# Gates, branch products and the merged sum of a three-layer block with tokens on the partitions

## The chip, the cores and the metric

The kernel runs on one core of a Trainium2 chip, as one program from load to store. Its time is device microseconds from the launch to the end of that core. Three runs are shown; the time of the kernel is their median. The profile is one more execution, in which every instruction of each engine was recorded: TensorE (PE, its weight loads PEld), VectorE (DVE), ScalarE (ACT), GpSimd (POOL) and SyncE (SP, which issues the DMAs).

## What is computed

256 tokens of width 1024 go through two layers of one kind and one of another. Each layer ends its mixing part in the same way: three branches of width 512, each multiplied by a branch matrix to width 1024, weighted by a sigmoid gate of width 1024 that is itself a product of the hidden state with columns of the input matrix, summed, and multiplied by an output matrix. Cut to that:

```
# layers 0 and 1 (hybrid_layer), h = rms_norm(x, ln_mix)
merge = (h @ w_in)[..., 3368:]                        # 3 x 1024 columns
gates = sigmoid(merge.reshape(B, S, 3, D) + b_merge)
merged = (gates[:, :, 0] * (o_nsa @ w_branch[0])
          + gates[:, :, 1] * (o_gla @ w_branch[1])
          + gates[:, :, 2] * (o_mem @ w_branch[2]))
x = x + merged @ w_out                                # then an MLP of width 4096

# layer 2 (hybrid_layer_2), h = x, no bias in the gates
gates = sigmoid((x @ w_in)[..., 5120:].reshape(B, S, 3, D))
mixed = sum over 3 branches of gates * (y @ w_branch)
out = layer_norm(ALPHA * x + mixed @ w_out, ln_g, ln_b)
```

All is float32. o_nsa, o_gla and o_mem are the results of a sparse attention, a gated linear attention and an attention over 256 memory tokens.

## The kernel before, in words

**Precision and weights.** Every large product is made from three float32r matmuls: each operand is split into a high and a low part, and high x high, high x low and low x high are summed in PSUM. Activations keep their parts in hh and hl (hidden state), oh and ol (branch results), mg (the merged sum). Weights arrive by DMA on SP's queue into one of four raw buffers of 1024 elements per partition (512 KB); `unit` (L441) issues the DMA, and `split` (L429) makes hi on ScalarE (L435; each sixth on POOL, L433) and lo on VectorE (L439). There are four hi and four lo buffers, so three units can lie ready while PE uses one.

**Two forms of a product.** `tok_major` (L489) has tokens on the partitions of the result: for each k (128 rows of the contraction) and each of the two token tiles, 128 tokens of the activation are stationary and up to 512 weight columns move; the two results fill two PSUM banks (acc, four in all). `transposed` (L503) has output columns on the partitions: for each of two blocks of 128 columns and each k, the 128 x 128 block of weights is stationary and the 256 tokens move; two blocks fill one PSUM bank. In the trace every matmul of both is at L188, the helper that records it; transposes are at L192.

**Order.** PE's order is written out by the program itself. A planned clock (clock, advanced at L187 and L191 by 1.69 or 0.425 ns per moving column) stands for PE's time. The attention parts are generators ("chains", L130 to L153) that yield the planned nanoseconds until their next step; `pump` runs those that are due after every three matmuls of `tok_major` or every six of `transposed`, so that their matmuls fall between those of the large products. `need` (L157) runs chains until a given k of an activation has been produced. The other engines' orders come from the framework's scheduler, and all semaphores too.

**The stage of the change.** For each branch (in layers 0 and 1 in the order 2, 1, 0) `gates_of` (L1125) makes the gate with four calls of `transposed`, each 256 columns: VectorE multiplies by the tokens' norm factor RB, laid along the free axis (L1130), and ScalarE does tanh with a bias per partition, CBH (L1134). Then `merge_branch` (L1137) makes the branch product in the same form. The first branch writes (gate + 1) x product into M (L1147); the later ones multiply in place (L1149) and POOL adds to M (L1150). In the last branch each quarter of M is split at once into mg by `hilo` (L522: high on ScalarE L527, low on VectorE L528), which the output projection `out_proj` (L1155) takes as its stationary operand: there output columns of M must lie on the partitions. In layer 2 (L1579 to L1593) the gate is a tanh straight from PSUM (L1585). There is one gate buffer and one M buffer.

Of the kernel before, what the change touches and what calls it, by code (L numbers as in the profile page):

```python
# [98 lines left out]
def block_kernel(ctx, tc, x_in, mem_in, positions, ln_mix, w_in, b_merge, nsa_q_norm, nsa_k_norm,  # L99
# [173 lines left out]
    def load_rows():  # L273
# [3 lines left out]
        rows(48, 48, b_merge.rearrange("l b (k p) -> (l b k) p", p=P))  # L277
# [53 lines left out]
    CBH = consts.tile([P, 48], F32, name="CBH")  # L331
# [4 lines left out]
    def late_cols():  # L336
        pt = PS()
        tr(pt[:, :128], ROWB, IDF)
        dve.tensor_copy(COL[:, 48:128], pt[:, 48:128])
        dve.memset(COL[0:16, 102:110], 1.0)  # L340
        dve.memset(COL[64:80, 102:110], 1.0)
        dve.tensor_scalar(CBH, COL[:, 48:96], 0.5, None, op0=OP.mult)
# [120 lines left out]
    def units(w2d, r0, nk, cols, paired=None, fine=False):  # L463
        n = sum(c1 - c0 for c0, c1 in cols)
        if paired:
            c0, c1 = cols[0]
            srcs = [(slice(64 * j, 64 * j + 64), 0, n,
                     w2d[256 * j:256 * j + 256, c0:c1].rearrange("(a d) n -> d a n", d=64)) for j in range(2)]
            h, lo = unit(srcs, 4, n)
            return [(h[:, j, :], lo[:, j, :]) for j in range(4)]  # L470
        per = max(1, 1024 // n)
# [17 lines left out]
    def tok_major(hh, hl, w2d, r0, nk, cols, fine=False):  # L489
        n = sum(c1 - c0 for c0, c1 in cols)  # L490
        ps = [ACC(), ACC()]
        ws = units(w2d, r0, nk, cols, None, fine)
# [26 lines left out]
    def v2(ps):  # L519
        return ps.rearrange("p (a b) -> p a b", a=2)  # L520
# [604 lines left out]
    def gates_of(l, b, hh, hl, RB):  # L1125
        g = B8("gate")
        for c in range(4):
            ps = transposed(hh, hl, w_in[l], 0, 8, 3368 + 1024 * b + 256 * c, ACC())
            tmp = T2("gtmp", (2, 256))
            dve.tensor_tensor(tmp, v2(ps), RB[:, None, :].to_broadcast([P, 2, 256]), op=OP.mult)  # L1130
            for j in range(2):
                cb = 2 * c + j
                bc = l * 24 + b * 8 + cb
                act(g[:, cb, :], tmp[:, j, :], AF.Tanh, scale=0.5, bias=CBH[:, bc:bc + 1])  # L1134
        return g

    def merge_branch(w2d, oT, g, M, last, mg, rows=None):  # L1137
        oh, ol = oT
        first = M is None
        if first:  # L1140
            M = B8("M")
        for c in range(4):
            ps = transposed(oh, ol, w2d, 0, 4, 256 * c, ACC(), rows)
            cs = slice(2 * c, 2 * c + 2)
            fl = lambda t: t[:, cs, :].rearrange("p a b -> p (a b)")
            if first:
                dve.scalar_tensor_tensor(fl(M), fl(g), 1.0, ps, op0=OP.add, op1=OP.mult)  # L1147
            else:
                dve.scalar_tensor_tensor(fl(g), fl(g), 1.0, ps, op0=OP.add, op1=OP.mult)  # L1149
                pool.tensor_tensor(fl(M), fl(M), fl(g), op=OP.add)  # L1150
                if last:
                    hilo(fl(mg[0]), fl(mg[1]), fl(M), 0.5)
# [525 lines left out]
```

## Time and profile before

| | |
|---|---|
| time, median of 3 runs | 1257.58 us (1254.6, 1257.58, 1258.07) |
| profiled execution, from its first to its last instruction | 1254.4 us |
| PE busy | 1234.7 us, 98% |
| DVE busy | 846.5 us, 67% |
| ACT busy | 596.6 us, 48% |
| POOL busy | 244.6 us, 19% |
| read from HBM | 208.74 MB, 167 GB/s over the span |

The profiled execution's span runs from its first to its last instruction and lies 3.2 us under the median. Layer 0 begins near 80 us, its gates near 145; its merge ends at 288.9 and the output projection starts there. Layer 1 has its gates from about 625 to 772, layer 2 from 1116 to 1227. A matmul's printed duration is longer than the distance from one to the next, because matmuls overlap; how fast PE goes is read from the starts.

### The profile page before, as it was taken

The page shows a single profiled execution, that of the slowest core. Times are in us where ns is not written, and L with a number is a line of the kernel's source. Part 1 is how long each engine was busy: PE and PEld are TensorE (multiplying, and loading weights), DVE is VectorE, ACT ScalarE, POOL GpSimd, SP SyncE. Part 2 cuts the span into 40 slices and gives each one's busy share as a digit, 9 for nine tenths or more (in the row PEclk, how much of TensorE's full clock was granted, in tenths as well). Part 3 has the DMA queues.
Part 4 walks back from the last instruction along what each step waited for, and adds up shares of the span by engine and source line. Part 5 has one row for each costly group of instructions (what it writes and reads, how often), then busy time and mean ns, then how long its engine had stood idle before and what let it go on. Part 6 is the DMA issues. An engine that isn't in the chain of part 4 may idle for free.

```text
span 1254.4 us, 21138 instructions
## 1 busy us (share of the span) xinstructions
PE 1234.7 (98%) x8317; PEld 1108.0 (88%) x8317; DVE 846.5 (67%) x1356; ACT 596.6 (48%) x956; POOL 244.6 (19%) x246
## 2 busy tenths in 40 slices
PE   8999999999999999999999999999999999999997
PEld 6897799998899899888799998989998988899996
DVE  5867878566754545567978566654545899956756
ACT  6567544444644444556644434544434343453532
POOL 2300320122112112200320023121211122111213
PEclk9999999999999999999999999999999999999999
DMA  8557533466566666656623566565665654445562
GB/s 269 177 157 203 155 101 102 137 185 199 185 185 185 189 183 196 184 153 173 191 68 112 155 167 190 177 193 179 198 187 171 202 155 137 153 135 169 179 219 74
DMA packets 165559, 211.00 MB, mean 168 GB/s; under 512 B 12065, under 2 KB 132277, under 8 KB 165460
## 3 DMA queue, kind: packets, MB, share of 16 engines
q1 hardware_dynamic: 165172, 209.49, 55.9%
q8 instruction: 65, 1.06, 0.3%
q0 software_dynamic: 288, 0.16, 0.1%
q14 instruction: 34, 0.28, 0.1%
HBM read 208.74 MB, written 1.05 MB: 167 GB/s over the span
## 4 chain that ended last, share of the span: by engine, by line
PE 84%; DVE 8%; POOL 2%; ACT 2%; issue 2%; DMA 0%; SPq 0%; POOLq 0%; ACTq 0%; DVEq 0%
PE acc L188 59%; PE psm L188 18%; PE psm L192 3%; PE pso L188 3%; DVE lo L439 3%; DVE b8x L1435 2%; POOL M L1150 2%; ACT hi L435 1%; PE acc L782 1%; ACT b8x L527 1%; DVE gate L1149 0%; DVE b8x L528 0%; DVE QB L1046 0%; ACT pexp L920 0%; DMA gtmp<-in_mem_norm 0%
## 5 line engine op out<-in xcount | busy, mean ns | idle before, releaser
L439 DVE TENSOR_TENSOR lo<-raw,hi 128x1024 fp32r<-128x1024 f32 (+1 forms) x359 | 451.5, 1261 | 264.0 <-ACT hi L435 203.5
L435 ACT ACTIVATE hi<-raw 128x1024 fp32r<-128x1024 f32 (+1 forms) x314 | 330.0, 1057 | 415.4 <-PE acc L188 254.7
L188 PE MATMUL acc<-hh,hi 128*128 128x256 f32 x960 | 278.7, 290 | 0.4 <-ACT hi L435 0.4
L188 PE MATMUL acc<-hh,lo 128*128 128x256 f32 x960 | 272.0, 283 | 1.7 <-DVE lo L439 1.6
L188 PE MATMUL acc<-hl,hi 128*128 128x256 f32 x960 | 271.9, 283 | 0.0
L188 PEld LDWEIGHTS acc<-hh,hi 128*128 128x128 f32 x960 | 184.0, 192 | 4.1 <-issue 2.5
L188 PEld LDWEIGHTS acc<-hh,lo 128*128 128x128 f32 x960 | 184.0, 192 | 2.3 <-DVE lo L439 2.3
L188 PEld LDWEIGHTS acc<-hl,hi 128*128 128x128 f32 x960 | 184.1, 192 | 1.1 <-DVE hl L528 0.2
L433 POOL TENSOR_SCALAR hi<-raw 128x1024 fp32r<-128x1024 f32 x55 | 67.0, 1219 | 477.8 <-PE acc L188 319.7
L188 PE MATMUL psm<-hh,hi 128*128 128x256 f32 x448 | 126.8, 283 | 0.0
L188 PE MATMUL psm<-hh,lo 128*128 128x256 f32 x448 | 126.8, 283 | 0.0
L188 PE MATMUL psm<-hl,hi 128*128 128x256 f32 x448 | 126.8, 283 | 0.0
L188 PE MATMUL acc<-hi,b8x 128*128 128x512 f32 (+1 forms) x336 | 104.0, 384 | 0.1
L188 PE MATMUL acc<-hi,oh 128*128 128x512 f32 x256 | 100.2, 391 | 0.0
L188 PE MATMUL acc<-lo,oh 128*128 128x512 f32 x256 | 99.8, 390 | 0.0
L188 PE MATMUL acc<-hi,ol 128*128 128x512 f32 x256 | 99.6, 389 | 0.0
L188 PE MATMUL acc<-hi,hh 128*128 128x512 f32 (+1 forms) x224 | 90.0, 402 | 0.0
L188 PE MATMUL acc<-lo,hh 128*128 128x512 f32 (+1 forms) x224 | 84.8, 378 | 2.2 <-DVE lo L439 2.2
L188 PEld LDWEIGHTS psm<-hl,hi 128*128 128x128 f32 x448 | 86.0, 192 | 0.5
L188 PEld LDWEIGHTS psm<-hh,hi 128*128 128x128 f32 x448 | 86.0, 192 | 0.5
L188 PEld LDWEIGHTS psm<-hh,lo 128*128 128x128 f32 x448 | 86.0, 192 | 0.0
L188 PE MATMUL acc<-hi,hl 128*128 128x512 f32 (+1 forms) x224 | 84.8, 378 | 0.0
(369 smaller groups left out, 2151.5 us busy)
## 6 DMA issues: line engine op xcount, KB each, us to landing
raw<-in_w_in SPq DMA_DIRECT2D x160, 512.0 KB
raw<-in_w_up SPq DMA_DIRECT2D x64, 512.0 KB
raw<-in_w_down SPq DMA_DIRECT2D x64, 512.0 KB
raw<-in_w_branch SPq DMA_DIRECT2D x28, 512.0 KB
raw<-in_w_out SPq DMA_DIRECT2D x24, 512.0 KB
raw<-in_cmp_w SPq DMA_DIRECT2D x32, 256.0 KB
raw<-in_mem_w_kv SPq DMA_DIRECT2D x15, 512.0 KB
raw<-in_w_branch SPq DMA_DIRECT2D x16, 256.0 KB
```

The lines of the kernel that those rows point to most:

```text
L188: nc.tensor.matmul(o, l, r, start=start, stop=stop, skip_group_check=True)
L192: nc.tensor.transpose(o, i, ident)
L433: pool.tensor_scalar(hi, raw, 1.0, 1.0, op0=OP.mult, op1=OP.mult)
L435: act(hi, raw, AF.Copy)
L439: dve.tensor_tensor(lo, raw, f32(hi), op=OP.subtract)
L527: act(hi, src, AF.Copy, scale=scale)
L782: nc.tensor.matmul(ph[32 * j:32 * j + 32, k * 256:k * 256 + 256], R[k][:, lp].rearrange("p a b -> p (a b)"), rv[:, j, :], start=q == 0, st ...
L1150: pool.tensor_tensor(fl(M), fl(M), fl(g), op=OP.add)
L1435: dve.scalar_tensor_tensor(CV[:, cb], GLU[:, cb, t:t + 256], CWT[:, cb, t:t + 1], CV[:, cb], op0=OP.mult, op1=OP.add)
```

## The change

Gates, branch products and M get the form of `tok_major`: tokens on the partitions, two halves of 512 columns instead of four calls of 256. `units` cuts the paired rows of the last branch's matrix into two units per half, so that units keep their size of 1024 elements. `gates_of` now takes the norm factor per partition (rsd) and loads b_merge, the same row for all 128 partitions and both token tiles, by a DMA on POOL's queue into the gate buffer itself; VectorE multiplies the PSUM by rsd and adds it in one step, and ScalarE does tanh in place. CBH and the rows of b_merge at the start go. In the last branch VectorE adds to M instead of POOL, and a new chain, `merged_transposed`, transposes each half of M on PE (four blocks of 128 x 128 per token tile) and splits it from PSUM into mg; `out_proj` finds through `need` which k of mg are planned. Layer 2 has the same, without bias.

```diff
     def units(w2d, r0, nk, cols, paired=None, fine=False):
         n = sum(c1 - c0 for c0, c1 in cols)
+        per = max(1, 1024 // n)
         if paired:
             c0, c1 = cols[0]
-            srcs = [(slice(64 * j, 64 * j + 64), 0, n,
-                     w2d[256 * j:256 * j + 256, c0:c1].rearrange("(a d) n -> d a n", d=64)) for j in range(2)]
-            h, lo = unit(srcs, 4, n)
-            return [(h[:, j, :], lo[:, j, :]) for j in range(4)]
-        per = max(1, 1024 // n)
+            res = []
+            for k in range(0, 4, per):
+                srcs = [(slice(64 * j, 64 * j + 64), 0, n,
+                         w2d[256 * j + 64 * k:256 * j + 64 * (k + per), c0:c1].rearrange("(a d) n -> d a n", d=64))
+                        for j in range(2)]
+                h, lo = unit(srcs, per, n)
+                res += [(h[:, j, :], lo[:, j, :]) for j in range(per)]
+            return res
...
-    def gates_of(l, b, hh, hl, RB):
-        g = B8("gate")
-        for c in range(4):
-            ps = transposed(hh, hl, w_in[l], 0, 8, 3368 + 1024 * b + 256 * c, ACC())
-            tmp = T2("gtmp", (2, 256))
-            dve.tensor_tensor(tmp, v2(ps), RB[:, None, :].to_broadcast([P, 2, 256]), op=OP.mult)
-            for j in range(2):
-                cb = 2 * c + j
-                bc = l * 24 + b * 8 + cb
-                act(g[:, cb, :], tmp[:, j, :], AF.Tanh, scale=0.5, bias=CBH[:, bc:bc + 1])
+    def gates_of(l, b, hh, hl, rsd):
+        g = B8("gate", shape=(2, 1024))
+        nc.gpsimd.dma_start(g, wrap(b_merge[l, b], [[0, P], [0, 2], [1, 1024]]))
+        for h in range(2):
+            hs = slice(512 * h, 512 * h + 512)
+            c0 = 3368 + 1024 * b + 512 * h
+            ps = tok_major(hh, hl, w_in[l], 0, 8, [(c0, c0 + 512)])
+            for tt in range(2):
+                gs = g[:, tt, hs]
+                dve.scalar_tensor_tensor(gs, ps[tt], rsd[:, tt:tt + 1], gs, op0=OP.mult, op1=OP.add)
+                act(gs, gs, AF.Tanh, scale=0.5)
         return g
+
+    def merged_transposed(M, h, mg, prog):
+        yield 1500.0
+        for tt in range(2):
+            pt = PS()
+            for j in range(4):
+                tr(pt[:, j * P:j * P + P], M[:, tt, 512 * h + j * P:512 * h + j * P + P], IDF)
+            ks, ts_ = slice(4 * h, 4 * h + 4), slice(tt * P, tt * P + P)
+            hilo(mg[0][:, ks, ts_], mg[1][:, ks, ts_], v4(pt), 0.5)
+            if tt == 0:
+                yield 800.0
+        prog[0] = 4 * h + 4
 
     def merge_branch(w2d, oT, g, M, last, mg, rows=None):
         oh, ol = oT
         first = M is None
         if first:
-            M = B8("M")
-        for c in range(4):
-            ps = transposed(oh, ol, w2d, 0, 4, 256 * c, ACC(), rows)
-            cs = slice(2 * c, 2 * c + 2)
-            fl = lambda t: t[:, cs, :].rearrange("p a b -> p (a b)")
-            if first:
-                dve.scalar_tensor_tensor(fl(M), fl(g), 1.0, ps, op0=OP.add, op1=OP.mult)
-            else:
-                dve.scalar_tensor_tensor(fl(g), fl(g), 1.0, ps, op0=OP.add, op1=OP.mult)
-                pool.tensor_tensor(fl(M), fl(M), fl(g), op=OP.add)
-                if last:
-                    hilo(fl(mg[0]), fl(mg[1]), fl(M), 0.5)
+            M = B8("M", shape=(2, 1024))
+        prog = [0]
+        if last:
+            ready[id(mg[0])] = (mg[0], prog)
+        for h in range(2):
+            hs = slice(512 * h, 512 * h + 512)
+            ps = tok_major(oh, ol, w2d, 0, 4, [(512 * h, 512 * h + 512)], False, rows)
+            for tt in range(2):
+                gs, ms = g[:, tt, hs], M[:, tt, hs]
+                if first:
+                    dve.scalar_tensor_tensor(ms, gs, 1.0, ps[tt], op0=OP.add, op1=OP.mult)
+                else:
+                    dve.scalar_tensor_tensor(gs, gs, 1.0, ps[tt], op0=OP.add, op1=OP.mult)
+                    (dve if last else pool).tensor_tensor(ms, ms, gs, op=OP.add)
+            if last:
+                start(merged_transposed(M, h, mg, prog))
         return M
...
         for bi, b in enumerate((2, 0, 1)):
-            g = B8("gate")
-            for c in range(4):
-                ps = transposed(hh, hl, w, 0, 8, 5120 + 1024 * b + 256 * c, ACC())
-                act(g[:, 2 * c:2 * c + 2, :], v2(ps), AF.Tanh, scale=0.5)
+            g = B8("gate", shape=(2, 1024))
+            for h in range(2):
+                c0 = 5120 + 1024 * b + 512 * h
+                ps = tok_major(hh, hl, w, 0, 8, [(c0, c0 + 512)])
+                for tt in range(2):
+                    act(g[:, tt, 512 * h:512 * h + 512], ps[tt], AF.Tanh, scale=0.5)
```

## Rows read from the trace of the kernel before

**Rows 1.** Part 1 of the page: busy time of each engine, its share of the span and its instructions.

```profile
PE 1234.7 (98%) x8317; PEld 1108.0 (88%) x8317; DVE 846.5 (67%) x1356; ACT 596.6 (48%) x956; POOL 244.6 (19%) x246
```

**Rows 2.** Busy time by stretch, in the stages of the change. Columns: the stretch, its length, then busy us (and instructions) of PE, PEld, DVE, ACT and POOL, the granted clock as a share of full, the share of the DMA engines, GB/s.

```profile
160.00:202.90 42.90, 42.53 (x321) 38.81 (x321) 34.99 (x88) 20.79 (x46) 8.49 (x14) 0.96 0.33 99
...
242.97:279.90 36.93, 36.93 (x310) 36.93 (x310) 22.93 (x22) 15.64 (x21) 8.85 (x6) 1.00 0.63 171
...
1151.00:1214.00 63.00, 63.00 (x527) 63.00 (x527) 41.89 (x44) 27.73 (x35) 11.45 (x8) 1.00 0.57 180
```

**Rows 3.** Who waited for whom over the whole span: total us, times, the longest. The first row is PE's largest, the second ScalarE's.

```profile
PE acc L188 <- DVE lo L439: 4.1, 4, 2.2
...
ACT hi L435 <- PE acc L188: 254.7, 149, 8.5
```

**Rows 4.** PE in order of time at the start of layer 0's output projection: start, us, what. "x2" is two matmuls taken together.

```profile
296.83 0.93 PE L188 MATMUL acc<-hi,b8x 128*128 128x512 f32 x2
297.60 0.40 PE L188 MATMUL acc<-lo,b8x 128*128 128x512 f32 x1
297.99 0.73 PE L188 MATMUL acc<-hi,b8x 128*128 128x512 f32 x2
298.56 0.39 PE L188 MATMUL acc<-lo,b8x 128*128 128x512 f32 x1
```

**Rows 5.** The chain of work that ended last, in order of time: start, us, engine, result, line and matmuls of an unbroken run. In this order: 512 moving columns (mem_kv and layer 0), 256 columns (gates of layer 0), 256 columns (MLP), 512 columns (MLP).

```profile
49.92 10.93 PE acc L188 x48
...
242.97 36.95 PE acc L188 x308
...
372.92 11.51 PE psm L188 x96
384.44 10.91 PE acc L188 x48
```

**Rows 6.** Groups of instructions by line and form: the branch products of three layers, one of their three matmuls.

```profile
L188 PE MATMUL acc<-oh,hi 128*128 128x256 f32 x288 | 83.1, 288 | 0.0
```

**Rows 7.** The same chain in order of time: four transposes between matmuls.

```profile
304.19 0.44 PE psm L192 x4
```

**Rows 8.** Groups of instructions by line and form: engine, out<-in, count, busy us and mean ns of one, idle time before and its releaser. Evacuations of gates and products, the adds to M, the split of M, and the splits of weights.

```profile
L439 DVE TENSOR_TENSOR lo<-raw,hi 128x1024 fp32r<-128x1024 f32 x353 | 445.6, 1266 | 260.8 <-ACT hi L435 200.3 <-POOL hi L433 59.0
...
L1150 POOL TENSOR_TENSOR M<-M,gate 128x512 f32<-128x512 f32 x24 | 43.2, 1802 | 90.8 <-DVE gate L1149 85.2 <-ACT hi L435 5.5
...
L1134 ACT ACTIVATE gate<-gtmp,CBH 128x256 f32<-128x256 f32 x48 | 22.2, 501 | 12.5 <-DVE gtmp L1130 12.4
...
L1130 DVE TENSOR_TENSOR gtmp<-acc,RB 128x512 f32<-128x512 f32 x24 | 16.4, 684 | 0.9 <-PE acc L188 0.9
L1149 DVE SCALAR_TENSOR_TENSOR gate<-gate,acc 128x512 f32<-128x512 f32 x24 | 16.3, 680 | 6.9 <-PE acc L188 6.9
...
L528 DVE SCALAR_TENSOR_TENSOR b8x<-M,b8x 128x512 fp32r<-128x512 f32 x12 | 9.4, 787 | 16.6 <-ACT b8x L527 16.6
...
L527 ACT ACTIVATE b8x<-M 128x512 fp32r<-128x512 f32 x12 | 7.6, 632 | 31.4 <-POOL M L1150 31.4
...
L1298 DVE TENSOR_TENSOR X<-X,acc 128x512 f32<-128x512 f32 x8 | 5.1, 679 | 0.0
```

**Rows 9.** DMAs that POOL issues, from the list of DMA issues (KB each, median us from issue to landing), and two single microseconds of layer 2 by stretch (columns as in rows 2).

```profile
DM<-const_d POOLq DMA_DIRECT2D x1, 96.0 KB, 4.4
...
CBT<-const_b POOLq DMA_DIRECT2D x1, 64.0 KB, 5.5
```

```profile
1216.00:1217.00 1.00, 1.00 (x11) 1.00 (x10) 1.00 (x1) 0.00 (x0) 0.97 (x1) 1.00 0.77 193
...
1218.00:1219.00 1.00, 1.00 (x11) 1.00 (x10) 1.00 (x3) 0.67 (x1) 0.00 (x0) 1.00 1.05 406
```

**Rows 10.** Layer 0, chains between gate matmuls, in order of time: PE from 155 to 182, then VectorE's steps that it reads, then two stretches of layer 0 and layer 1 (columns as in rows 2).

```profile
155.19 3.64 PE L188 MATMUL psm<-KB,b8x 128*128 128x16 f32 x32
...
159.36 0.28 PE L188 MATMUL acc<-hl,hi 128*128 128x256 f32 x1
159.48 0.28 PE L188 MATMUL acc<-hh,lo 128*128 128x256 f32 x1
...
161.84 0.41 PE L188 MATMUL acc<-hl,hi 128*128 128x256 f32 x1
162.05 0.41 PE L188 MATMUL acc<-hh,lo 128*128 128x256 f32 x1
...
176.88 0.82 PE L192 MATMUL psm<-CF,pexp 128*128 128x128 f32 x6
178.06 0.68 PE L188 MATMUL psm<-QB,b8x 128*128 128x128 f32 x4 [0.37 <-DVE a L1059]
...
181.98 0.76 PE L188 MATMUL pso<-pts,n 128*64 128x256 f32 x3
```

```profile
176.96 0.60 DVE L925 TENSOR_SCALAR pexp<-pexp,r 128x256 f32<-128x256 f32 x2
...
179.57 0.55 DVE L940 COPY pts<-psm 128x384 f32<-128x384 f32 x1
```

```profile
160.00:180.00 20.00, 19.63 (x143) 18.15 (x143) 17.42 (x49) 8.91 (x25) 7.67 (x12) 0.92 0.24 80
640.00:660.00 20.00, 20.00 (x161) 18.78 (x159) 19.07 (x52) 10.22 (x26) 7.24 (x12) 1.00 0.31 96
```

More of the change, by code (lines that the diff above doesn't have):

```diff
@@ L275, in rows @@
             nc.sync.dma_start(ROWB[r0:r0 + n, :], src)
-        rows(48, 48, b_merge.rearrange("l b (k p) -> (l b k) p", p=P))
         rows(96, 2, gla_norm)
@@ L330, in block_kernel @@
     dve.tensor_copy(COL[:, 32:48], pt[:, 32:48])
-    CBH = consts.tile([P, 48], F32, name="CBH")
     GQK = consts.tile([P, 2], F32, name="GQK")
@@ L338, in late_cols @@
         tr(pt[:, :128], ROWB, IDF)
-        dve.tensor_copy(COL[:, 48:128], pt[:, 48:128])
+        dve.tensor_copy(COL[:, 96:128], pt[:, 96:128])
         dve.memset(COL[0:16, 102:110], 1.0)
         dve.memset(COL[64:80, 102:110], 1.0)
-        dve.tensor_scalar(CBH, COL[:, 48:96], 0.5, None, op0=OP.mult)
         dve.tensor_tensor(GQK, COL[:, 98:100], COL[:, 100:102], op=OP.mult)
@@ L487, in units, with tok_major @@
         return res
-    def tok_major(hh, hl, w2d, r0, nk, cols, fine=False):
+    def tok_major(hh, hl, w2d, r0, nk, cols, fine=False, paired=None):
         n = sum(c1 - c0 for c0, c1 in cols)
         ps = [ACC(), ACC()]
-        ws = units(w2d, r0, nk, cols, None, fine)
+        ws = units(w2d, r0, nk, cols, paired, fine)
         for k, (wh, wl) in enumerate(ws):
@@ L1276, in layer @@
         for b in (2, 1, 0):
-            g = gates_of(l, b, hh, hl, RB)
+            g = gates_of(l, b, hh, hl, rsd)
             if b == 2:
```

## The prediction

> **What bounds the kernel now.** I read the busy times of the page first [rows 1]: TensorE works 98% of the span, the next engine, VectorE, 67%. So the question is what the change does to TensorE's own time, and after that whether something else makes TensorE wait. The table by stretches says the same for the stages that the change touches [rows 2]: in the pure gate stretches (242.97 to 279.9 in layer 0, 1151 to 1214 in layer 2) PE is busy for the whole stretch, while VectorE has 22.9 of 36.9 and 41.9 of 63.0 us. In 160 to 202.9, where attention chains run between the gate matmuls, VectorE has 35.0 of 42.9 us and PE still only 0.4 us of idle time. The waits agree [rows 3]: all that PE waited for splits (VectorE's low parts) is 4.1 us in four places of the whole span, while ScalarE, which makes the high parts, waits 254.7 us for PE to free a buffer. Weights are there before PE wants them; PE's rate sets the time.
>
> The chain of waits shows POOL's adds of 2.1 us at the end of each merge. That is a side chain: at the same time PE goes on with matmuls. Where it touched PE shows in PE's own order of time [rows 4]: six matmuls from 296.83 to 298.79 take 1.96 us, which at the pitch below would be 1.36, so 0.6 us was lost there.
>
> **Part 1, the matmuls.** The price of one is its pitch in an unbroken run, not its printed duration (matmuls overlap). 96 with 256 moving columns take 11.51 us, 119.9 ns each; 308 in a gate stretch 36.95 us, 120.0 ns each; 48 with 512 moving columns take 10.91 us, 227.3 ns, or 10.93 with hidden states stationary, 227.7 ns [rows 5]. So two narrow ones (239.8) cost 12.5 ns more than the wide one that does the same columns: about 13 ns go with each matmul whatever its width, and the change halves their number. The counts: a gate block of 256 columns is 8 k x 2 blocks x 3 products = 48 matmuls, 4 blocks x 3 branches x 3 layers = 36 blocks, 1728 matmuls. A branch product has 4 k, so 24 x 36 = 864, three times the 288 of the row [rows 6]. 2592 matmuls x 119.9 ns = 310.8 us become 1296 x 227.3 = 294.6 us: **-16.2 us**, of which 5.4 per layer. All lies on PE, which has no idle time there, so it counts in full unless a wait takes its place.
>
> The Trainium skill gives another price: TensorE: Matmul & The Clock Gate, section Back-to-back issue gap, has a warm isolated gap of N/2.4 + 2.5 ns. By it a pair costs 218.3 and the wide one 215.8 ns, only 3.2 us over 1296 pairs. The rows stand 10.7 and 11.5 ns above that rule, so the measured pitches decide.
>
> **Part 2, the transposes.** The sum M now has tokens on partitions and needs 4 transposes x 2 halves x 2 token tiles = 16 per layer, 48 in all. Four in the midst of matmuls take 0.44 us, 0.11 us each [rows 7]: **+5.3 us**, all on PE.
>
> **Part 3, the evacuations.** Per branch, VectorE did four gate products of 0.68 us and does four scalar_tensor_tensor of 0.68 us; the merge products stay four at 0.68 [rows 8]. ScalarE's eight gate activations of 0.50 become four of about 0.6 us, 1.6 us less. In the last branch four adds move from POOL (1.8 us mean) to VectorE (0.68 by the form nearest to it, L1298): 2.7 us more VectorE per layer. Hidden as long as VectorE keeps up: it has 38% of layer 0's pure gate stretch free [rows 2]. One weight unit now feeds 12 x 227.3 = 2.73 us of PE and costs VectorE 1.27 us; number and size of the units, and SP's DMAs, stay as they were, and k outermost frees each unit after 2.73 us. Cost taken as nothing. The b_merge rows and CBH lie in the first stage, ahead of their use: nothing.
>
> **Part 4, the hand-over to the output projection.** Before, half-chunks of M went POOL, ScalarE, VectorE; now VectorE, PE, ScalarE, VectorE, and PE stands in order, so it can wait. The planner runs the transposes after 1500 and 800 ns of its clock, looked at after each group of three matmuls: after the 4th group (4 x 0.68 = 2.73 us behind the last product) and two groups and 0.45 us later (4.5 us). The four VectorE steps need 0.2 + 4 x 0.68 = 2.9 us, the first pair 1.6; each split that goes between adds 1.27. So the first M tile is there at 1.6 to 4.1, the second at 2.9 to 5.4: a wait of 0 to 1.4 us per half, 0 to 8.4 over six. I take the near end with one split in between, 0.1 each, 0.6 in all. Then k=4 of the projection needs the second half's high and low parts: transposes end near 5.0, ScalarE 0.63 and VectorE 0.79 [rows 8] give 6.6, up to 9 with a split ahead on both; PE comes there at 6.4 to 7.0. 0 to 2 us per layer; I take 0.5, 1.5 in all. The 0.6 us of rows 4 goes.
>
> **Part 5, the bias by DMA.** gates_of for layers 0 and 1 now loads b_merge as 1 MiB through POOL's queue into the only gate buffer, six times. It must wait until the last reader of that buffer is done, and VectorE's first gate step of the branch waits for it; behind that step stand VectorE's splits, and behind those PE. For branch 0 the last reader is POOL's add. With t the end of branch 1's last product: two VectorE steps and two POOL adds give t + 5.2 (0.9 + 2 x 2.1). The trace of before has only small DMAs on that queue, 96 KB landing in 4.4 us and 64 KB in 5.5 [rows 9]. 1 MiB more takes 2.6 us at the best rate of a single microsecond (406 GB/s), and 8.4 us if it gets half of the engines: 193 GB/s at a share of 0.77 is 251 GB/s, half of that 125. Landing t + 12.2 to 18.0. The first half's PSUM is full at t + 10.9, so VectorE stands still for 1 to 7 us. PE then has three split units ahead (four buffers, one in use), 8.2 us, and runs dry at t + 19.1; VectorE needs 2.7 us (two gate steps, one split) first, so PE waits only if the landing is past t + 16.4: 0 to 1.6 us per layer, 3.2 in all. I take 0. Branch 1 waits for VectorE alone (t + 1.6) and lands 3.6 us sooner; branch 2's buffer is free long before. POOL has little else queued behind, a split of 1.2 us in six.
>
> DMA: Bandwidth & Descriptors of the Trainium skill, section Anatomy of one DMA, fits such a DMA at 2.0 us + bytes/436e3, which an estimate makes 4.4 us for 1 MiB, landing at t + 9.6, before it is wanted. The 96 KB row took 4.4 where that fit says 2.2, so the sum goes by the rows.
>
> **Part 6, the chains.** In 145 to 243 and 625 to 721 two of three gates run between attention steps whose places are counted in the planner's clock. That clock prices 2 x 108.8 the same as 217.6, so the order stays, but real time between two steps shrinks by 5%. Some slack is thin: 0.37 us of PE idle behind a masked copy at 178.06, while the probabilities for the transposes of 176.88 were ready at 177.56 [rows 10]; elsewhere 1.9 us (an attention copy done at 180.12 is read at 181.98). Between nothing and all 3.6 us of these two branches is lost per layer, 0 to 7.2; I take 0.5 per layer, 1.0, since PE idles only 0.4 of 42.9 us there. The granted clock also fell in layer 0, to the lower level of 1.2 GHz from 159.7 to about 163 (pitch 0.21 instead of 0.12 us), after 32 matmuls of 16 columns; its mean is 0.92 in 160 to 180, and 1.00 in 640 to 660 of layer 1 [rows 10]. That loses some 1.6 us; it may vanish or come twice: -1.6 to +1.6, taken as 0.
>
> **The sum.** -16.2 + 5.3 + 0.6 + 1.5 - 0.6 + 0 + 1.0 = -8.4 us. On the profiled span of 1254.4 that is 1246.0; the median of the three runs is 3.2 us above the span (1257.58), so I forecast **1249.2 us**. Least: -16.2 + 5.3 - 0.6 - 1.6 = -13.1, 1244.5.
>
> **Rivals.** (a) The hand-overs and chains eat the gain: half of their bounds (4.2 + 3.0 + 3.6) in place of my 3.1 gives -0.7, 1256.9. For it: VectorE at 82% in 160 to 202.9, four dependent steps before each transpose. Against: PE idle next to nothing there now. (b) A wide matmul costs in this place what two narrow ones do (239.8 ns): nothing gained, 5.3 paid for transposes, the rest covered, 1262.9; the pitches of rows 5, from other places, speak against it. By the gap rule of the Trainium skill (TensorE: Matmul & The Clock Gate, Back-to-back issue gap) 3.2 would be gained and the time be 1259.7, within 0.3%. (c) **Slower:** the bias holds VectorE until PE runs dry. It decides from a landing at t + 16.4 on, for branch 0 and branch 1 of two layers, four places; each microsecond beyond is one of PE. At a quarter of the engines' rate (63 GB/s, 16.7 us) branch 0 lands at t + 26.3 and branch 1 at 22.7, a loss of 2 x (9.9 + 6.3) = 32 us, 1282. The kernel is slower by 0.3% once these four places lose 12.2 us together. Against it: peaks of 406 GB/s show that the engines have room beside the 171 GB/s of this stage.
>
> **How the numbers follow.** Forecast 0.70 (own range 1244 to 1253.5), (a) 0.19, (b) 0.03, (c) 0.08. About 0.3%, 3.8 us, is what a measurement of this kernel can tell from no change. Faster is the forecast's share, 0.70; same (a), 0.19; slower (b) and (c), 0.11. Range 1244 to 1257.5: it takes in the least sum and (a), and leaves out (c), (b) and a sliver below.
>
> **What would show it.** Right: PE groups acc<-oh,... of 288 turn into 144 with 512 columns at a pitch of 0.227, gate stretches last 5% less, 48 new transposes at 0.11 us, PE at 98% still. Wrong: PE waiting for VectorE's M or for high and low parts at the start of the projection (part 4); VectorE idle before the gate step with the DMA as releaser for over 7 us (part 5); more PE idle in 145 to 243 (part 6); a pitch above 0.23 for the new matmuls (part 1).

## The result, and the profile after

The kernel after takes **1249.97 us** (median of 4 runs, 1246.2 to 1252.55), the kernel before 1256.99 in the same comparison (4 runs, 1254.6 to 1258.07): ratio **0.9947**, 95% interval 0.9926 to 0.9968. The kernel after was measured a second time with the first experiments: 1248.67 (6 runs), ratio 0.9932 [0.9919, 0.9946]. So the gain is 7.0 and 7.7 us where 8.4 was forecast. The profiled executions differ more than the medians: spans of 1254.4 before and 1244.4 after, 10.0 us. What lies between 10 and 7 us is taken up in point 7 below.

TensorE bounds the kernel as before. Part 1 of the page after, to be held against [rows 1]:

```profile
PE 1224.2 (98%) x7069; PEld 1042.5 (84%) x7069; DVE 853.3 (69%) x1367; ACT 590.0 (47%) x932; POOL 226.4 (18%) x240
```

1248 instructions fewer on PE are the 1296 saved matmuls and the 48 added transposes; VectorE has 7 us more to do. The chain of waits, in order of time (start, us, engine, result, line, matmuls), has the new pitch:

```profile
178.32 1.39 PE acc L188 x6
...
202.11 5.51 PE acc L188 x24
...
240.85 40.85 PE acc L188 x180
...
1110.23 24.71 PE acc L188 x108
```

In the unbroken stretches 40.85/180 = 226.9 ns and 24.71/108 = 228.8 ns, where [rows 5] had 120.0 for half the columns. In the first two rows, between chain steps, it is 231.7 and 229.6 ns: a little more. Where [rows 2] had busy times by stretch, after has (the stretch, its length, busy us and instructions of PE, PEld, DVE, ACT and POOL, granted clock, DMA share, GB/s):

```profile
160.00:202.90 42.90, 42.13 (x231) 33.53 (x230) 34.51 (x87) 19.61 (x41) 7.72 (x14) 0.97 0.29 87
240.85:280.00 39.15, 39.15 (x174) 32.36 (x174) 25.91 (x25) 14.99 (x17) 10.84 (x8) 1.00 0.73 204
1110.23:1134.00 23.77, 23.77 (x105) 19.69 (x106) 12.27 (x13) 11.98 (x14) 3.46 (x2) 1.00 0.55 162
```

PE is still busy for the whole of the pure gate stretches, and VectorE still has a third or more of them free. The waits of PE (total us, times, longest), against [rows 3]:

```profile
PE acc L188 <- DVE lo L436: 3.8, 3, 2.2
PE psm L192 <- DVE kss L583: 2.1, 1, 2.1
PE psm L188 <- ACT ck L824: 1.4, 2, 1.1
...
PE psm L188 <- DVE a L1060: 0.8, 1, 0.8
...
PE psm L188 <- ACT pts L939: 0.4, 1, 0.4
```

No wait for the sum M is among them, and none for its high and low parts. Three rows have grown: the wait for kss, in the stage ahead of layer 0, was 1.3 us before (point 7), and the last two, for steps of the attention chains, were 0.4 and nothing (point 6). The new evacuations, by line and form (busy us, mean ns), against [rows 8]:

```profile
L1168 POOL TENSOR_TENSOR M<-M,gate 128x512 f32<-128x512 f32 x12 | 21.2, 1785 | 28.0 <-DVE gate L1167 28.0
L1135 DVE SCALAR_TENSOR_TENSOR gate<-acc,xrs,gate 128x512 f32<-128x512 f32 x24 | 17.3, 747 | 9.6 <-PE acc L188 5.0 <-DMA gate<-in_b_merge 4.3
L1167 DVE SCALAR_TENSOR_TENSOR gate<-gate,acc 128x512 f32<-128x512 f32 x24 | 15.3, 680 | 0.0
...
L1168 DVE TENSOR_TENSOR M<-M,gate 128x512 f32<-128x512 f32 x12 | 7.9, 702 | 0.0
```

The product step takes the 0.68 us that was predicted, the gate step 0.75 and the add 0.70 where 0.68 was put for both. The first row is POOL's adds of the middle branch; the last branch's are on VectorE now. The load of the bias, from the list of DMA issues (KB each, median us to landing):

```profile
gate<-in_b_merge POOLq DMA_DIRECT2D x6, 1024.0 KB, 7.6
```

The six took 6.3 to 9.5 us; the landing at t + 12.2 to 18.0 of the prediction implies 7.0 to 12.8. The Trainium skill (DMA: Bandwidth & Descriptors, Anatomy of one DMA) had given an estimate of 4.4 us; no load came in that time, and the measured number decides.

### The profile page after: what moved, and what is told of

It is laid out like the page before. It is cut to its first block, busy times and chain, and to the rows that moved or that the text cites. A ratio compares the mean times of both kernels' runs of the same rounds, so it can differ in the third digit from the quotient of the medians.

```text
span 1244.4 us, 18619 instructions
## 1 busy us (share of the span) xinstructions
PE 1224.2 (98%) x7069; PEld 1042.5 (84%) x7069; DVE 853.3 (69%) x1367; ACT 590.0 (47%) x932; POOL 226.4 (18%) x240
## 4 chain that ended last, share of the span: by engine, by line
PE 89%; DVE 6%; ACT 2%; issue 1%; POOL 1%; DMA 1%; SPq 0%; POOLq 0%; DVEq 0%; ACTq 0%
PE acc L188 64%; PE psm L188 18%; PE psm L192 3%; PE pso L188 3%; DVE b8x L1453 2%; DVE lo L436 2%; PE acc L783 1%; ACT hi L432 0%; DMA raw<-in_mem_w_kv 0%; DVE QB L1047 0%; ACT pexp L921 0%; DVE a L1060 0%; DMA gtmp<-in_mem_norm 0%; POOL b8x L1032 0%; POOL QB L1047 0%
## 5 line engine op out<-in xcount | busy, mean ns | idle before, releaser
L436 DVE TENSOR_TENSOR lo<-raw,hi 128x1024 fp32r<-128x1024 f32 (+1 forms) x359 | 448.1, 1252 | 268.3 <-ACT hi L432 221.2
L188 PE MATMUL acc<-hi,hh 128*128 128x512 f32 (+1 forms) x512 | 206.9, 404 | 0.0
L188 PE MATMUL acc<-lo,hh 128*128 128x512 f32 (+1 forms) x512 | 197.9, 386 | 2.2 <-DVE lo L436 2.2
L188 PE MATMUL acc<-hi,hl 128*128 128x512 f32 (+1 forms) x512 | 198.3, 387 | 0.0
L188 PEld LDWEIGHTS acc<-hi,hh 128*128 128x128 f32 x512 | 97.0, 189 | 21.3 <-issue 4.8
L188 PEld LDWEIGHTS acc<-hi,hl 128*128 128x128 f32 x512 | 96.6, 189 | 19.6
L188 PEld LDWEIGHTS acc<-lo,hh 128*128 128x128 f32 x512 | 96.9, 189 | 19.0 <-DVE lo L436 2.9
L188 PE MATMUL acc<-hh,hi 128*128 128x256 f32 x384 | 111.7, 291 | 0.0
L188 PE MATMUL acc<-hh,lo 128*128 128x256 f32 x384 | 108.7, 283 | 1.3 <-DVE lo L436 1.3
L188 PE MATMUL acc<-hl,hi 128*128 128x256 f32 x384 | 108.8, 283 | 0.0
L188 PEld LDWEIGHTS acc<-hi,oh 128*128 128x128 f32 x400 | 75.2, 188 | 15.0 <-issue 0.3
```

The source lines that it names most:

```text
L188: nc.tensor.matmul(o, l, r, start=start, stop=stop, skip_group_check=True)
L436: dve.tensor_tensor(lo, raw, f32(hi), op=OP.subtract)
```

## Experiments

The theory before the runs: the width is worth 12.5 ns per saved matmul, the transposes cost 5.3 us, hand-over and bias are covered. Its rivals: something else than the width made the gain (the layout), or the covered parts cost time that no wait shows.

**The kernel after once more**, as the partner of the next three.

> The changed kernel once more, as the partner of the three others on this chip. Theory W (width: each matmul costs some 13 ns on top of its columns, the change has 1296 fewer, 16.2 us, and pays 5.3 for 48 transposes; everything else is hidden) and the rivals say the same here: a span near 1244.4, 10 us under the kernel before, ratio 0.992 to 0.996.

Measured: 1248.67 us, ratio 0.9932 [0.9919, 0.9946]. The next three are held against this run. The experiments were measured in three groups, and the kernel before took 1256.10 to 1256.67 us in them (medians), so kernels of different groups can be compared to within about half a microsecond.

**Width undone, layout kept.** Each wide matmul of gates and products becomes two narrow ones.

```
-mm3(ps[tt][:, :n], hh[:, k, ts_], hl[:, k, ts_], wh, wl, k == 0, k == nk - 1)
+x, y = hh[:, k, ts_], hl[:, k, ts_]
+for l_, r_, s0, s1 in ((x, wh, k == 0, False), (x, wl, False, False), (y, wh, False, k == nk - 1)):
+    for q in (slice(0, 256), slice(256, 512)):
+        mm(ps[tt][:, q], l_, r_[:, q], ...)
```

> The changed kernel, but each matmul of 512 columns in gates and branch products is issued as two of 256 with the same stationary block; layout, order of weights, evacuations and transposes stay. Theory W: 1296 more matmuls at 12.5 ns: +16.2 us in full, +13 if the parts between the chain steps give only 1.6 of 3.0 us per layer as the trace of the changed kernel suggests: span 1257 to 1261, slower than the kernel before by 3 to 6. Rival L (the gain comes from the layout: k outermost frees each weight unit earlier, ScalarE has less to do): about 0, span 1244 to 1247.

Measured: 1266.12 us, ratio 1.0071 [1.0059, 1.0083], 17.45 us above the kernel after. The chain of waits has the same stretches as above, with twice as many matmuls:

```profile
245.01 43.19 PE acc L188 x360
...
1124.84 26.11 PE acc L188 x216
```

43.19 us where the wide form takes 40.85, 120.0 ns each. The width is the gain; the layout by itself (this run against the kernel before) loses 9.75 us, the transposes among it. The span, 1264.6 us, lies above the 1257 to 1261 that were expected; part of that is the stage ahead of layer 0, which took 53.0 us here and 49.3 in the profile from which the expectation was made (point 7). By the isolated gap that the Trainium skill gives (TensorE: Matmul & The Clock Gate, Back-to-back issue gap) an estimate for the cut is 3.2 us; this run does not agree.

**Transposes left out.**

```
-pt = PS()
-for j in range(4):
-    tr(pt[:, j * P:j * P + P], M[:, tt, ...], IDF)
-hilo(..., v4(pt), 0.5)
+hilo(..., v4(M[:, tt, 512 * h:512 * h + 512]), 0.5)
```

> Leaves out the 48 transposes of M: high and low parts are split straight from M in SBUF (the projection then works on numbers in the wrong order, same amount of work). Theory W: 48 x 0.11 = 5.3 us less than the changed kernel, span near 1239.1. Rival H (the hand-over waits, or the transposes fill time that PE would stand still anyway): less than 2 us if they are hidden, more than 7 us if PE also waits for M there.

Measured: 1244.66 us, ratio 0.991 [0.989, 0.9931], 4.0 us below the kernel after where 5.3 was expected. In its trace layer 2 (from the run of 371 matmuls to PE's last) lasts 266.4 us against 268.3, 1.9 for 16 transposes, which makes 5.7 for 48. Why the medians show 4.0 is not shown; the mean granted clock of its six runs was lower (0.992 against 0.994), and in its trace the stage ahead of layer 0 took 55.2 us.

**Gates alone in the new form**, with the merge of the kernel before.

```
 # merge_branch as in the kernel before:
+for c in range(4):
+    ps = transposed(oh, ol, w2d, 0, 4, 256 * c, ACC(), rows)
+    ...
+        pool.tensor_tensor(fl(M), fl(M), gs, op=OP.add)
```

> Gates wide with tokens on the partitions and the bias by DMA as in the changed kernel; branch products, adds on POOL and split of M as in the kernel before, no transposes (gate and product then meet in different layouts, so the numbers are not the reference's; amount of work the same). Theory W: 18 halves x 2 calls... 18 blocks of 512 columns x 0.60 us = 10.8 us less than before, about 2 of them lost between chain steps: span near 1245.5. Rival L with k outermost only in the gates: the same sign, but no figure from the pitch; under 5 us would speak for it.

Measured: 1250.64 us, ratio 0.9952 [0.9934, 0.9969], 5.7 us below the kernel before, where some 8.8 were expected. Layer 2 became 3.75 us shorter by the trace, as its 288 saved matmuls should (3.6); layers 0 and 1 gained less. This, and the 1.3 and 1.6 us that the trace of the kernel after lacks in the stretches with chains of layers 0 and 1, asked for the two runs with breaks below.

**Bias left out.**

```
-nc.gpsimd.dma_start(g, wrap(b_merge[l, b], ...))
-dve.scalar_tensor_tensor(gs, ps[tt], rsd[:, tt:tt + 1], gs, op0=OP.mult, op1=OP.add)
+dve.tensor_scalar(gs, ps[tt], rsd[:, tt:tt + 1], None, op0=OP.mult)
```

> The kernel after, but in layers 0 and 1 the load of the b_merge rows into the gate buffer and the adding of that bias are left out (the gate step multiplies by the row's factor alone); the gates of these layers so lack their bias. Theory (VectorE's wait of 4.3 us for this load, seen once in the profile of the kernel after, is covered by split units already made, so the load costs the end nothing): the time of the kernel after, 1249 to 1250 us, within 3 us; VectorE's wait for the load disappears and PE's order in layers 0 and 1 stays as it was. Rival (the load shares the DMA engines with the weights, or VectorE's standing still costs PE something that no PE wait shows): 2 to 6 us less, most of it in the gate stretches of layers 0 and 1, where the kernel after gained less than the pitches say.

Measured: 1247.19 us (4 runs, 1246.58 to 1250.26), ratio 0.9941 [0.9924, 0.9959]. The intervals overlap with the kernel after's. In its trace layer 0 lasts 59.94 us from the start of the run of 180 matmuls (branch 1's product, then branch 0's gates) to the run of 48 that begins at 300.79 in the kernel after, the same as there; in layer 1 it is 80.51 us from that start to the MLP, against 80.92. So branch 0's load costs PE 0 to 0.4 us per layer, and for it the theory holds. The median is 1.5 to 2.8 us below the kernel after's, and the rival, that the load shares the DMA engines with the weights, has a case in the stage ahead of layer 0 (point 7).

**Bias loaded twice**, one load behind the other into the same buffer.

```
 nc.gpsimd.dma_start(g, wrap(b_merge[l, b], [[0, P], [0, 2], [1, 1024]]))
+nc.gpsimd.dma_start(g, wrap(b_merge[l, b], [[0, P], [0, 2], [1, 1024]]))
```

> The kernel after with the load of the b_merge rows issued twice in a row into the same buffer, so that VectorE's gate step gets its bias later; nothing is left out. One load took 6.3 to 9.5 us from issue to landing, and branch 0 of layer 1 landed at t + 14.4 (t the end of branch 1's last product). Theory (PE runs dry only past t + 16.4): the second load lands 6 to 10 us later, t + 20 to t + 24 for branch 0, and PE waits 4 to 8 us there in each of two layers; branch 1 lands 3.6 us sooner and costs 0 to 4 us: 8 to 24 us more than the kernel after, 1258 to 1274 us, with PE waiting for VectorE's low or ScalarE's high parts in both layers. Rival (the two loads run beside each other and land little later, or the cover in front of PE is longer than the 16.4 us of the prediction): within 3 us of the kernel after.

Measured: 1266.2 us, ratio 1.0089 [1.0065, 1.0113], 16 us above the kernel after. VectorE's order of time shows the gate step of branch 0 in layer 0 and 1 (start, us; in brackets the idle time before and what ended it):

```profile
275.92 1.41 DVE L1136 SCALAR_TENSOR_TENSOR gate<-acc,xrs,gate 128x512 f32<-128x512 f32 x2 [11.89 <-DMA gate<-in_b_merge]
```

```profile
760.91 1.41 DVE L1136 SCALAR_TENSOR_TENSOR gate<-acc,xrs,gate 128x512 f32<-128x512 f32 x2 [12.42 <-DMA gate<-in_b_merge]
```

And PE's in layer 0, behind it:

```profile
272.40 0.39 PE L188 MATMUL acc<-hi,hh 128*128 128x512 f32 x1
278.52 0.80 PE L188 MATMUL acc<-lo,hh 128*128 128x512 f32 x1 [5.73 <-DVE lo L436]
279.11 0.63 PE L188 MATMUL acc<-hi,hl 128*128 128x512 f32 x1
279.54 0.63 PE L188 MATMUL acc<-hi,hh 128*128 128x512 f32 x1
...
282.81 0.40 PE L188 MATMUL acc<-hi,hl 128*128 128x512 f32 x1
```

Branch 1's product ends, and branch 0's gates begin on PE, at 253.36: that is t. The first load is issued at 258.36 = t + 5.0, the bias is there at 275.9 = t + 22.6, PE ran dry at 272.79 = t + 19.4 and went on 2.6 us after the landing. Layer 1 is the same (t is 737.81, dry at t + 19.4, 6.27 us). The prediction had t + 19.1 and 2.7 us: the cover and its edge are confirmed from the far side. Branch 1 landed late too (VectorE waited 5.8 us for it in layer 1), but PE didn't wait there. The two waits make 12.0 of the 16 us. Most of the rest is in the rows behind the wait: some nine matmuls at a pitch of 0.43 us in place of 0.23, the lower level of the clock (1.2 GHz), 1.8 us at each place.

**The last branch's adds back on POOL.**

```
-(dve if last else pool).tensor_tensor(ms, ms, gs, op=OP.add)
+pool.tensor_tensor(ms, ms, gs, op=OP.add)
```

> The kernel after with the last branch's adds of the merged sum put back on POOL, where the kernel before had them; nothing is left out. POOL's adds took 1.8 to 2.1 us where VectorE's take 0.74. Theory (the transposes are given a place 2.7 to 4.5 us behind the last product, and the sum was ready 0.3 us ahead of them): two adds of some 2 us in a row make the second tile of a half ready 2 to 3 us later, so PE waits for M at the transposes of each half, 1 to 2.5 us in six places: 6 to 15 us more, 1256 to 1265 us. Rival (the projection's and the product's other work lies between, and POOL is early enough): under 3 us more.

Measured: 1251.82 us (7 runs), ratio 0.9971 [0.9959, 0.9984], 1.9 to 3.2 us above the two medians of the kernel after. The waits of PE that are new in it:

```profile
PE acc L188 <- DVE b8x L529: 0.7, 2, 0.4
...
PE psm L192 <- POOL M L1168: 0.2, 1, 0.2
```

A few tenths, late at the transposes once and at the projection twice. The rival was right or nearly so (under 3 us; 1.9 to 3.2 measured): POOL is nearly early enough, and moving the adds to VectorE is worth some 2 to 3 us, not the 6 to 15 of my theory.

**Transposes right behind the product.**

```
-yield 1500.0
+yield 100.0
 ...
-    yield 800.0
+    yield 100.0
```

> The kernel after with the two delays that the planner puts ahead of each half's transposes cut from 1500 and 800 to 100 each, so that the transposes come right behind the product in PE's order; nothing is left out. Theory (PE stands in order, and the sum M needs 1.6 us for the first and 2.9 us for the second token tile after the last product, one split of 1.27 us more where it goes between): PE waits 1 to 3 us per half for M, six halves, 6 to 18 us more than the kernel after, 1256 to 1268 us, and the hand-over's near-zero cost is the work of the delays. Rival (PE's work between the last product and the first transposes is not what hides the steps): within 3 us of the kernel after.

Measured: 1253.15 us (10 runs), ratio 0.9982 [0.9967, 0.9998], 3.2 to 4.5 us above the kernel after. PE now waits for the sum:

```profile
PE psm L192 <- DVE M L1168: 2.7, 5, 1.5
```

So the delays are what hides VectorE's steps; the waits are worth 2.7 us, less than the 6 to 18 expected, since four halves wait 0.2 to 0.5 us, one 1.5 and one not at all. Neither range held: the theory's cause was right, its size was not.

**Width undone between the chains alone**: branches 2 and 1 of layers 0 and 1, the same edit as above with `cut=b != 0`.

> The kernel after with each 512-column matmul cut into two of 256 columns, but only in the two branches of layers 0 and 1 that run between the attention chains' steps: 576 more matmuls, nothing left out. Theory (also between the steps a matmul pays about 12.5 ns whatever its width): 576 x 12.5 = 7.2 us more than the kernel after, 1256 to 1258 us. Rival (between the steps PE waits for the chain or loses to the switch from one run to the next, and the width is worth little there; the profile of after gained 3.1 us in these two stretches where 6.0 to 7.2 were expected): 1.5 to 3.5 us more, 1251 to 1253 us.

Measured: 1256.45 us (12 runs, 1248.93 to 1259.26), ratio 0.9995 [0.9981, 1.0009], 6.5 to 7.8 us above the kernel after (the profiled run is the fastest of the twelve). So the width is worth most of its price between the chains too, and my rival falls. The runs spread over 10 us: the fastest three had a mean granted clock of 0.995 or 0.996, the slowest three 0.991. The trace gives a figure without that spread: from the first run of 48 matmuls to the end it has 1198.55 us without a fall of the clock in layers 0 and 1, the kernel after 1195.0 to 1195.1 with one fall there of about 1.9 us (point 7), so 5.4 us more.

**Runs broken on purpose.** In layer 2, where no chain runs, two transposes behind each 6 wide matmuls (in the kernel after) or each 12 narrow ones (in the kernel before), 48 breaks in both.

```
+if brk:
+    for j in range(2):
+        nc.tensor.transpose(pb[:, j * P:j * P + P], IDF, IDF)
```

> The kernel after with two transposes of the identity put behind each six wide matmuls of the gates of layer 2, 48 interruptions in a stretch that had none (their results are read by nothing but one small copy per half). The transposes themselves cost about 0.11 us each, 10.6 us. Theory (a run of wide matmuls that is interrupted pays some 80 ns at its first matmul, as after a chain's step): the matmuls of the stage grow by 48 x 80 = 3.8 us beside that, to 14 or 15 us in all. Rival (the loss after a chain's step is the wait for the chain's result): 10.6 us and no more.

> The kernel before with two transposes of the identity put behind each twelve narrow matmuls of the gates of layer 2, 48 interruptions (their results are read by nothing but one small copy per block). Theory (an interruption costs a run the same, whatever the width, some 80 ns): 14 to 15 us more than the kernel before, as in the kernel after with as many interruptions, so that short runs take nothing from the gain of the wide form. Rival (the wide form loses more at each interruption, 30 ns or more): under 13 us here.

One run each, 1265.6 and 1267.42 us, so they are read by their traces. Layer 2 (from the run of 371 matmuls to PE's last) grew from 268.3 to 280.3 us in the wide kernel, 12.0, and from 272.4 to 282.75 in the narrow one, 10.3. The wide kernel's chain of waits, and PE's order of time in it:

```profile
1133.93 1.40 PE acc L188 x6
1135.55 1.39 PE acc L188 x6
```

```profile
1135.17 0.38 PE L505 MATMUL psm<-CF 128*128 128x128 f32 x2
1135.31 0.47 PE L188 MATMUL acc<-hi,hh 128*128 128x512 f32 x1
1135.62 0.39 PE L188 MATMUL acc<-lo,hh 128*128 128x512 f32 x1
1135.85 0.40 PE L188 MATMUL acc<-hi,hl 128*128 128x512 f32 x1
```

The narrow kernel's chain of waits, and PE's order of time:

```profile
1165.40 1.44 PE acc L188 x12
1167.06 1.44 PE acc L188 x12
```

```profile
1160.07 0.38 PE L517 MATMUL psm<-CF 128*128 128x128 f32 x2
1160.20 0.36 PE L188 MATMUL acc<-hh,hi 128*128 128x256 f32 x1
1160.40 0.28 PE L188 MATMUL acc<-hl,hi 128*128 128x256 f32 x1
1160.52 0.28 PE L188 MATMUL acc<-hh,lo 128*128 128x256 f32 x1
```

Over 14 periods further on the mean is 1.610 us wide (1159.61 to 1182.15) and 1.654 narrow (1160.44 to 1183.59). Without a break the same work takes 6 x 226.9 ns = 1.361 and 12 x 120.0 = 1.440. So a break costs the wide form 0.249 us and the narrow form 0.214; over the layer, 12.0 and 10.3 us by 48, 0.250 and 0.215. The first matmul pays about 80 ns in both (0.31 for 0.227, 0.20 for 0.120); the wide ones behind it stay at 0.23 us (1135.62 to 1135.85), 4 to 5 ns over the unbroken pitch, the narrow ones don't. The wide form loses **35 ns more at each break**, and no chain was there to wait for. Narrow_breaks' rival (30 ns or more, under 13 us) held, and of wide_breaks' theory its sign: the loss of a short run is in the run, but 12.0 us, not 14 to 15. The 0.22 us that were put for two transposes held the first matmul's delay already: they take 0.14 us here (1135.17 to 1135.31), and the 80 ns behind them make the rest.

## Why the prediction was right

The forecast was 1249.2 us; 1249.97 and 1248.67 were measured. The mechanism is the predicted one: fewer, wider matmuls on an engine that is never idle, less the transposes. The closeness of the number is in part luck, as the terms show:

1. **The matmuls (-16.2): right.** The pitch is 226.9 to 228.8 ns, predicted 227.3. Undoing the width alone cost 17.45 us by the medians; 5.6 us in layer 2 by the trace (273.9 against 268.3), where 5.4 is the term. What the 13 ns per matmul consist of is not shown: every matmul has a weight load of its own in these traces (PE and PEld both count 7069), and no run separates the two.
2. **The transposes (+5.3): right.** Left out, layer 2 is 1.9 us shorter (1.8 expected).
3. **The evacuations (0): right.** The gate step's 0.75 us makes VectorE 1.6 us longer; PE waits 3.8 us for low parts, before 4.1.
4. **The hand-over (+0.6 + 1.5 - 0.6): the two costs were not there.** In VectorE's order of time the pair of adds of layer 0's first half begins at 279.77 and takes 1.48 us, and PE's four transposes begin at 281.54 without a wait:

```profile
279.77 1.48 DVE L1168 TENSOR_TENSOR M<-M,gate 128x512 f32<-128x512 f32 x2
```

```profile
281.30 0.39 PE L188 MATMUL acc<-hi,ol 128*128 128x512 f32 x1
281.54 0.60 PE L192 MATMUL psm<-CF,M 128*128 128x128 f32 x4
```

   0.3 us of slack. The near end of the bounds (0 and 0) was the right one; early_tr shows that the cover is real and thin. The saving was larger than 0.6. From the run of 308 (after: 180) to the projection's run of 48, layer 0 went from 61.66 to 59.94 us and layer 1 from 60.98 us (to its run of 69) to 60.35; the 192 saved matmuls and 16 transposes make -0.6 of each. So 1.1 and 0.0 us (with the 0.4 of point 5 in it) are left for the hand-over, and in layer 2 another 0.4 (-4.1 in place of -3.6): about **-1.5** in all, where the sum had +1.5.
5. **The bias (0): right for branch 0, for the reason given; overlooked for branch 2.** In the profile VectorE waited for it once, 4.3 us in layer 1, and PE lost at most 0.4 us there; loaded twice, it costs 16 us. Rival (c), that the load starves PE, had the right mechanism; it needed a landing past t + 16.4, and the latest lay at about t + 14.9 (landed at 741.4, t is 726.5). Of branch 2 the prediction says only that its buffer is free long before. So its load in layer 0 starts while the weights of the stage ahead of the layer arrive; point 7 has what follows.
6. **The chains (+1.0): the right sign, about a third of the size.** Between chain steps, 240 of the matmuls saved in each of layers 0 and 1 should give 3.0 us. The stretches went from 94.72 to 93.02 us (148.25 to 242.97, after 147.83 to 240.85) and from 92.53 to 91.17 (628.52 to 721.05, after 624.57 to 715.74): 1.3 and 1.6 us are missing, **2.9** in all. The cause that the prediction named is part of it: PE's wait behind the masked copy, 0.37 us at 178.06 in [rows 10], became 0.77, and a wait of 0.40 for the copied probabilities (pts) appeared at 652.52 in layer 1, together 0.8 us. The rest is what the prediction did not have and the broken runs show: a cost of the short run itself, 35 ns more per break for the wide form. About 30 breaks lie between chain steps in each of layers 0 and 1, 60 x 35 ns = 2.1 us. That the breaks of the chains cost what those made on purpose cost is an inference.
7. **The stage ahead of layer 0, and the clock (±1.6, taken as 0).** With points 4 and 6 corrected the sum is -16.2 + 5.3 - 1.5 + 2.9 = -9.5. The layers of both profiled executions of the kernel after meet it; the medians do not, and the difference lies ahead of the layers. The chain of waits of the kernel before (its first run of 48, at 49.92, is in [rows 5]), then of the first and of the second profile of the kernel after:

```profile
304.63 9.65 PE acc L188 x48
...
973.49 44.77 PE acc L188 x371
...
1116.16 26.11 PE acc L188 x216
```

```profile
49.31 10.93 PE acc L188 x48
...
300.79 9.62 PE acc L188 x48
...
967.53 44.78 PE acc L188 x371
```

```profile
53.04 10.89 PE acc L188 x48
...
302.60 9.62 PE acc L188 x48
...
971.15 44.77 PE acc L188 x371
...
1113.84 24.71 PE acc L188 x108
```

   | from ... to, us | before | after, first profile | after, second profile |
   |---|---|---|---|
   | start to the run of 48 | 49.92 | 49.31 | 53.04 |
   | to the run of 48 in layer 0's projection | 254.71 | 251.48 | 249.56 |
   | to the run of 371 | 668.86 | 666.74 | 668.55 |
   | to layer 2's gates | 142.67 | 142.70 | 142.69 |
   | to the end | 138.24 | 134.17 | 134.16 |
   | all but the first row | 1204.48 | 1195.09 | 1194.96 |

   The last row gives -9.4 and -9.5 us. In each of the three the clock falls once in layers 0 and 1: in layer 0 near 160 in the first two, in layer 1 near 640 in the third, which is the 1.8 to 1.9 us between their rows. The first row varies. In the second profile PE waits 3.1 us for VectorE (kss), 1.3 in the kernel before, and the clock falls behind that wait (0.91 in 20 to 40). VectorE is late there because ScalarE, whose high part it needs, waits longer for the weights of w_in; some 10 us earlier POOL has issued branch 2's bias load. ScalarE before, then ScalarE and POOL in the second profile of the kernel after:

```profile
27.15 1.06 ACT L435 ACTIVATE hi<-raw 128x1024 fp32r<-128x1024 f32 x1 [0.78 <-DMA raw<-in_w_in]
```

```profile
29.39 1.06 ACT L432 ACTIVATE hi<-raw 128x1024 fp32r<-128x1024 f32 x1 [3.28 <-DMA raw<-in_w_in]
```

```profile
19.76 0.79 POOL L1128 DMA_DIRECT2D gate<-in_b_merge  x1 [0.46 <-issue]
```

   All ten traces with this load have it issued between 18.5 and 20.7 us. In eight of them ScalarE waits 2.4 to 4.4 us for those weights, and PE's next run (60 matmuls) begins at 33.3 to 35.8; in the other two, the kernel after's first profile among them, it waits 1.6 us or not at all, and the run begins at 31.3 and 31.9. In the three traces without the load (before, narrow_breaks, no_bias) ScalarE waits 0.8, 0.4 and 0 us, and the run begins at 32.5, 31.5 and 33.4. This points to a collision of the early load with the weights, which part 5 of the prediction left out when it counted a buffer that is free long before as no cost. From these starts I put it at some 1 to 3 us, an estimate; the medians lack 1.7 to 2.4 of what the layers gain. No run moves this load alone, so the price is not shown. The clock also falls in 20 to 40 in two of the three traces without the load, so it is not the only cause of a late first stage.

So the forecast met the median by errors that cancel: the hand-over 3.0 us too dear, the chains 1.9 us too cheap, the stage ahead of layer 0 counted as unchanged. The forecast was also set against 1257.58 us, the median of three runs; the partners of the two measurements took 1256.99 and 1256.37. Rival (a), that hand-overs and chains eat the gain, took 2.9 of its 10.8 us, all in the chains. Rival (b), that a wide matmul costs two narrow ones, is refuted by cut_256.

## What to carry to other kernels

On a TensorE that is never idle, price a change of width by the pitch of unbroken runs of either width in the same trace, and count what short runs lose separately: here 13 ns per matmul at 256 and at 512 columns, some 80 ns per break and 35 ns more for the wide form. For a transfer that only just hides, work out the point at which the engine behind it runs dry; that point can be tested by making the transfer late on purpose. For a transfer whose buffer is free early, ask also what it meets when it starts at once: here it was the weights of the stage ahead of layer 0. Where a gain is under 1% and executions differ, compare them stage by stage: the layers of two executions agreed within 0.2 us here, while the stage ahead of them differed by 3.7.

## What the runs showed of the hardware that was not expected

- **The clock falls at a few places, in some executions and not in others, and not every fall costs time.** In the kernel after's first profile the stretch 160 to 180 has a granted clock of 0.93; the second has 1.00 there and falls in 20 to 40 (0.91) and 620 to 640 (0.94). Such a fall in the layers costs 1.8 to 1.9 us (nine matmuls at 0.43 us). Both profiles also fall to 0.91 in 1020 to 1040, where the kernel before does not, and the stage around it lasts 142.7 us in all three: VectorE is busy for the whole stretch there and sets the pace. The row of the kernel before, then of the kernel after:

```profile
1020.00:1040.00 20.00, 17.76 (x77) 13.41 (x77) 20.00 (x32) 6.48 (x8) 5.41 (x2) 1.00 0.52 157
```

```profile
1020.00:1040.00 20.00, 18.00 (x72) 13.73 (x73) 19.99 (x41) 7.08 (x15) 2.98 (x1) 0.91 0.51 158
```

  So the mean granted clock of an execution (0.9956 over 44 runs of the kernel before, 0.9939 over 10 of the kernel after) does not by itself say what time was lost. What decides a fall in one execution stays open.
- **A wait can cost its length and the clock behind it.** In bias_twice 5.7 us of idle PE were followed by matmuls at the lower level that cost 1.8 us; the stretch 270 to 290 has a granted clock of 0.83.
- **The first matmul after a break starts late**, by some 80 ns, at either width, and a wide run stays 4 to 5 ns per matmul above its unbroken pitch for at least the five matmuls seen.
